# A mixer's masks and mean shift as matmuls, its state decay on ScalarE, and a last norm by pairs

## The chip, the cores and the metric

The kernel runs on one core of one Trainium2 chip. The metric is device time in microseconds (us) of one execution, the median over runs. Engines are named as the profile names them: PE (TensorE matmul), PEld (its weight load), DVE (VectorE), ACT (ScalarE), POOL (GpSimd), SP (SyncE, which here only issues DMAs).

## The reference

One inference step of a decoder trunk with two layers, for a prompt of 256 tokens and 8 decode streams of one token: 264 columns, model width 1024.

```python
def layer(x, ...):                                   # post-norm, DN_ALPHA = sqrt(2)
    h = layer_norm(DN_ALPHA * x + 0.5 * swiglu(x, f1g, f1u, f1d), ln1_g, ln1_b)
    mix, s_new, c_new, p_new = mixer(h, s0, conv_buf, pool_buf, ...)
    h = layer_norm(DN_ALPHA * h + mix, ln2_g, ln2_b)
    return layer_norm(DN_ALPHA * h + 0.5 * swiglu(h, f2g, f2u, f2d), ln3_g, ln3_b)
def mixer(h, ...):
    qkv, z, b_raw, a_raw, p = split(h @ w_in)        # q,k,v: 4 heads of 128 each; p: 4 groups of 128
    q, k, v = causal_conv(qkv, conv_buf, conv_w)     # 4 taps, then silu
    o, s_new = gated_delta(q, k, v, beta, g, s0)     # decay exp(g); dec = exp(gc_i - gc_j) for i >= j
    o_dn = rms_norm(o) * onorm_g * silu(z)
    y = (window_means(p, 2/4/8/16) - p) @ pool_w * pool_scale
    return concat([o_dn, y]) @ w_out, s_new, ...
```

The decode streams carry a 128x128 state for each head and stream: s_new = decay * s0 + (outer product).

## The kernel before

All activations lie transposed, channels on partitions and the 264 tokens along the free axis, in tiles of 128 channels. Weights come as fp32 and are used in two parts: for each 128x1024 piece ACT writes a rounded copy (`whi`, L178) and DVE the rest (`wlo`, L183); `mm3` (L219 to L221) multiplies in three matmuls per 128x128 block. Three slots each hold `whi` and `wlo`, so a piece is split when PE has left the piece three before it. PE runs in the order of the code; for the other engines a scheduler sets the order when the program is built, and each engine then works strictly in that order, waiting where a semaphore is not there yet.

A layer is: FFN (L428 on), norm, mixer (L495 on), norm, FFN, norm. The mixer, in PE's order:

- the k projections, the projections q0 and p3 with the small one for beta and decay, then q1, p2, q2, p1, `map3`, q3, the three `pdiff` products, p0, `map2`, v0, `map1`, v1, the transposes of k (`psq`), v2, `map0`, the mean shift `psh`, v3 with the scores (`psc`).
- `p_tile(g)` (L590) copies a pool projection into `ext`, and POOL builds the window sums `wsum` by g+1 additions of shifted copies (L604). `wsum` and `ext` have two buffers each: an addition must wait until the sum two before it is read.
- `p_map(g)` (L609) makes the row `dm` (mean less token) in four DVE steps, L615, L617, L619 and L620; its `finish`, called map3 to map0 here, multiplies it with the pool weights (`py`, L624). For g=3 alone `dm` is made without high priority.
- the decays: DVE makes four masked tiles `gm` (L702), PE sums them over tokens in `pdiff` (L706), ACT takes exp into `DT` (L708), and POOL multiplies `DT` by the causal mask or a factor (L710, L711).
- `conv` (L520): one ACT and three DVE steps per q, k or v tile (L525); `k_raw` keeps the k projections until then.
- then seven levels that invert a triangular matrix (`pP`, `pUt`, `pR` on PE, `QW`, `V`, `T` on DVE and ACT, `N` on POOL at L1008). Between the steps of a level PE does the z projections (`pz`), reads of the decode state (`psk`) and the first half of the output projection (`pop`). `decode_conv` (L776) prepares the decode keys, `less_shift` (L324) subtracts the mean shift from the residual X on POOL, `stack` (L902) splits the decode keys into the tile `parts` (L905 on ACT, L906 on POOL) and transposes it on PE (`pst`, L908), and POOL decays the state `S` (L885).

The lines of the pool means and of the decay masks that the rest of the text names:

```python
                    nx = mp.tile([P, EXT], F32, name="wsum", tag="wsum", bufs=2)
                    nc.gpsimd.tensor_add(nx[:, lo + d:], cur[:, lo + d:], cur[:, lo:EXT - d])
...
                with tc.high_priority() if g < 3 else nullcontext():
                    nc.vector.scalar_tensor_tensor(dm[:, 16:SEQ], cur[:, 31:15 + SEQ], 1.0 / wd, ext[:, 31:15 + SEQ],
                                                   ALU.mult, ALU.subtract)
                    nc.vector.scalar_tensor_tensor(dm[:, SEQ:], csm[:, :, 15], 1.0 / wd, smp[:, :, 15],
                                                   ALU.mult, ALU.subtract)
                    nc.vector.tensor_mul(dm[:, 0:16], cur[:, 15:31], cst[:, C_INV + 16 * g:C_INV + 16 * g + 16])
                    nc.vector.tensor_sub(dm[:, 0:16], dm[:, 0:16], ext[:, 15:31])
...
                        nc.vector.tensor_mul(gm, lemask, gp[:, i, t, :].unsqueeze(2).to_broadcast([P, H, P]))
```

The third step is the last that reads `wsum` (`cur`); the fourth reads `ext` alone.

After the last layer `output` (L379) subtracts the mean (`dmu`), multiplies by rstd and the gain, adds the bias, and stores y.

Of the kernel before, what the change touches and what calls it, by code (L numbers as in the profile page):

```python
# [25 lines left out]
H = 4  # L26
# [7 lines left out]
XB = 5  # L34
SB = 3
IDLE = 18

# [52 lines left out]
def trunk(ctx: ExitStack, tc: tile.TileContext, a: dict):  # L90
# [16 lines left out]
    onr = cpool.tile([P, P], F32R, name="onr")  # L107
    gto = cpool.tile([P, 2, P], F32R, name="gto")

    kq = cpool.tile([P, H * P], F32R, name="kq")  # L110
# [128 lines left out]
    class Norm:  # L239
# [78 lines left out]
        def centre(self):  # L318
            p = psa.tile([P, T], F32, name="psh", tag="ax")
            for k in range(2):  # L320
                nc.tensor.matmul(p, onr, HH[:, k, :], start=k == 0, stop=k == 1)
            self.set_shift(p, 4.0)

        def less_shift(self, after):  # L324
            for m in range(KD):
                with behind(after):
                    nc.gpsimd.tensor_sub(X[:, m, :], X[:, m, :], self.shift)  # L327

# [50 lines left out]
        def output(self, out):  # L379
            for m in (0, 1, 2, 3, 6, 7, 4, 5):  # L380
                y = X[:, m, :]
                (nc.gpsimd if m > 3 else nc.vector).tensor_sub(y, y, self.dmu)
            prev = None
            for m in (0, 1, 2, 3, 6, 4, 5, 7):
                y = X[:, m, :]
                if m > 5:
                    nc.gpsimd.tensor_mul(y, y, self.rstd)
                    with behind(prev):
                        nc.scalar.activation(y, y, AF.Identity, scale=self.g(m), bias=self.b(m))
                else:  # L390
                    nc.vector.scalar_tensor_tensor(y, y, self.g(m), self.rstd, ALU.mult, ALU.mult)
                    if m > 3:
                        nc.vector.tensor_scalar(y, y, self.b(m), None, ALU.add)
                    else:
                        prev = nc.scalar.activation(y, y, AF.Identity, bias=self.b(m))
                n = {4: 0, 6: 0, 5: 2, 7: 2}.get(m, 1)
                if n:
                    nc.sync.dma_start(out=out[(m - n + 1) * P:(m + 1) * P, :].rearrange("(m p) t -> p m t", p=P),
                                      in_=X[:, m - n + 1:m + 1, :])

# [94 lines left out]
    def mixer(l, src, norm, xstack):  # L495
        with tc.tile_pool(name="mp", bufs=1, reuse_waits="tile") as mp:
# [39 lines left out]
            def k_raw(ps):  # L536
                y, bias = src.settle(ps)
                raw = mp.tile([P, T], F32, name="raw", tag="tmp", bufs=4)
                nc.scalar.activation(raw, y, AF.Identity, bias=bias)
                return raw  # L540
# [25 lines left out]
            def q_tile(j, ps=None):  # L566
                W.ahead(2)
                conv(ps or product(W.get(), "q"), 4 + j)
                cq[j] = ct[4 + j]
# [39 lines left out]
            def p_map(g):  # L609
                ext, smp, cur = pend[g]  # L610
                wd = 2 << g
                dm = mp.tile([P, T], F32, name="dm", tag="tmp", bufs=4)
                csm = cur[:, 15 + SEQ:].rearrange("p (b i) -> p b i", i=16)
                with tc.high_priority() if g < 3 else nullcontext():
                    nc.vector.scalar_tensor_tensor(dm[:, 16:SEQ], cur[:, 31:15 + SEQ], 1.0 / wd, ext[:, 31:15 + SEQ],  # L615
# [6 lines that stand above are left out]
                def finish():  # L622
                    py = psa.tile([P, T], F32, name="py", tag="ax")
                    nc.tensor.matmul(py, pw[:, g, :], dm, start=True, stop=True)  # L624
                    yp = mp.tile([P, T], F32, name="yp", tag="tmp", bufs=4)
# [11 lines left out]
            p_tile(3, pp)  # L637
            for j in range(4):
                conv(kr[j], j)
            ck = ct[0:4]  # L640

# [3 lines left out]
            with tc.high_priority():  # L645
# [70 lines left out]
            v_tile(0, e_last)  # L716
            p_map(1)()

# [20 lines left out]
            for t in range(2):  # L739
                sumsq(ck, ssk, ke, t)  # L740
            v_tile(2, e_last)
# [4 lines left out]
            p_map(0)()  # L746
            norm.centre()
# [16 lines left out]
            v_tile(3, e_last, [nothing] * 2 + [lambda h=h: score(h) for h in range(H)])  # L764

            state = {}

# [8 lines left out]
            def decode_conv():  # L776
# [8 lines left out]
                nc.gpsimd.tensor_sub(lo, kq_in, hi.bitcast(F32))  # L785
                state["dsq"] = nc.gpsimd.tensor_mul(dsq[:, 8:12], dec[:, 0:4], dec[:, 4:8])
                nc.scalar.dma_start(out=a["o_ctail"][l], in_=stg)
# [56 lines left out]
            sk = dtile("sk", 2 * HB)  # L844
            skt = mp.tile([P, T], F32, name="skt", tag="tmp", bufs=4)[:, 0:P]

# [7 lines left out]
            def s_read(x):  # L854
# [18 lines left out]
                def last():  # L873
# [27 lines left out]

            def stack(i, src_, dst):  # L902
# [3 lines left out]
                nc.gpsimd.tensor_sub(pt[:, :, 2 - i, :], hb(src_), pt[:, :, 0, :])  # L906
                p = psa.tile([P, P], F32, name="pst", tag="ax")
                nc.tensor.transpose(p, parts[i], ident())  # L908
# [46 lines left out]
            def w_pool(m):  # L955
# [6 lines left out]
                def step(k):  # L962
                    mm3(ps, w, 4 * (m % 2) + k, mh[4 + k], ml[4 + k], k == 0, k == 3)

# [105 lines left out]
            for x in range(2):  # L1070
                pack(2, x)
            norm.less_shift(state["dsq"])
            for x in range(2):
# [14 lines left out]
            def stack_u():  # L1088
                stack(1, us, ust)
                s_prep(0)  # L1090
                s_prep(1)

            def w_level():
# [3 lines left out]
            fillers = [lambda: z_level(1, decode_sums, s_read(0), nothing),  # L1097
                       lambda: z_level(2, lambda: stack(0, dk, kst), s_read(1), nothing),
                       lambda: z_level(3, nothing, (s_turn, nothing), norms), q_level, w_level]
# [178 lines left out]
    def constants_in():  # L1278
        nc.sync.dma_start(out=sm, in_=a["small"])
        nc.sync.dma_start(out=cst, in_=a["cst"])  # L1280
        nc.scalar.activation(onr, cst[:, C_M1024:C_M1024 + P], AF.Copy)
        nc.scalar.activation(gto, cst[:, C_ONE:C_ONE + 2 * P].rearrange("p (i n) -> p i n", i=2), AF.Copy)
        for t in (*parts, kq.bitcast(F32)):
# [106 lines left out]
```

## Time and profile before

| | |
|---|---|
| three runs | 1083.95, 1085.35, 1085.57 us; median 1085.35 |
| profiled execution | 1089.43 us; its span 1087.6 us |
| PE busy in the span | 1046.0 us (96%) |
| DVE, ACT, POOL busy | 765.6, 581.8, 205.9 us |
| mean granted PE clock | 0.989 of full speed |

The span runs from the first to the last instruction; the profiled execution's own time holds 1.8 us more. An idle engine costs time only where the engine that ends the stretch waits for it, so the table alone says only that PE seldom waits.

### The profile page before, as it was taken

The page shows a single profiled execution, that of the slowest core. Times are in us where ns is not written, and L with a number is a line of the kernel's source. Part 1 is how long each engine was busy: PE and PEld are TensorE (multiplying, and loading weights), DVE is VectorE, ACT ScalarE, POOL GpSimd, SP SyncE. Part 2 cuts the span into 40 slices and gives each one's busy share as a digit, 9 for nine tenths or more (in the row PEclk, how much of TensorE's full clock was granted, in tenths as well). Part 3 has the DMA queues.
Part 4 walks back from the last instruction along what each step waited for, and adds up shares of the span by engine and source line. Part 5 has one row for each costly group of instructions (what it writes and reads, how often), then busy time and mean ns, then how long its engine had stood idle before and what let it go on. Part 6 is the DMA issues. An engine that isn't in the chain of part 4 may idle for free.

```text
span 1087.6 us, 20766 instructions
## 1 busy us (share of the span) xinstructions
PE 1046.0 (96%) x8410; PEld 1030.9 (95%) x8410; DVE 765.6 (70%) x1226; ACT 581.8 (53%) x1016; POOL 205.9 (19%) x248
## 2 busy tenths in 40 slices
PE   8999999998899999999999999999899999999995
PEld 8999999988798999999999999999788999999994
DVE  5555567899789955557785555778996898555554
ACT  6444445666447744444574444466664476444432
POOL 0000012244940000003200000322467300000132
PEclk9999999999999999999999999999999999999997
DMA  8554444732234355544725545565331345455441
GB/s 306 187 192 172 179 172 184 290 130 83 97 133 169 127 190 189 194 169 180 265 86 194 179 172 192 180 236 195 130 119 41 154 165 188 166 190 194 155 156 40
DMA packets 35872, 183.24 MB, mean 168 GB/s; under 512 B 6848, under 2 KB 12608, under 8 KB 15552
## 3 DMA queue, kind: packets, MB, share of 16 engines
q1 hardware_dynamic: 28704, 175.19, 44.6%
q10 hardware_dynamic: 7072, 6.72, 1.8%
q8 instruction: 66, 1.08, 0.4%
q14 instruction: 30, 0.25, 0.1%
HBM read 175.18 MB, written 6.72 MB: 167 GB/s over the span
## 4 chain that ended last, share of the span: by engine, by line
PE 82%; DVE 10%; ACT 3%; POOL 2%; issue 1%; DMA 1%; ACTq 0%; DVEq 0%
PE pd L219 8%; PE pd L221 8%; PE pd L220 8%; PE pu L220 8%; PE pu L219 8%; PE pu L221 8%; PE pg L220 7%; PE pg L219 7%; PE pg L221 7%; DVE wlo L183 2%; POOL X L327 1%; DVE c L525 1%; ACT X L367 1%; DMA wraw<-in_f_gu 1%; PE pout L220 1%
## 5 line engine op out<-in xcount | busy, mean ns | idle before, releaser
L183 DVE TENSOR_TENSOR wlo<-wraw,whi 128x1024 fp32r<-128x1024 f32 (+1 forms) x301 | 369.9, 1231 | 203.8 <-ACT whi L178 203.0
L178 ACT ACTIVATE whi<-wraw 128x1024 fp32r<-128x1024 f32 (+1 forms) x301 | 312.5, 1041 | 318.7 <-issue 116.9
L219 PE MATMUL pd<-gh,whi 128*128 128x264 f32 x704 | 200.6, 285 | 0.0
L221 PE MATMUL pd<-gh,wlo 128*128 128x264 f32 x704 | 200.2, 284 | 0.0
L220 PE MATMUL pd<-gl,whi 128*128 128x264 f32 x704 | 199.1, 283 | 0.0
L219 PE MATMUL pg<-HH,whi 128*128 128x264 f32 x632 | 179.8, 284 | 1.2 <-ACT whi L178 1.2
L221 PE MATMUL pg<-HH,wlo 128*128 128x264 f32 x632 | 179.6, 284 | 0.3 <-DVE wlo L183 0.3
L219 PE MATMUL pu<-HH,whi 128*128 128x264 f32 x632 | 179.5, 284 | 0.0
L220 PE MATMUL pg<-HL,whi 128*128 128x264 f32 x632 | 179.4, 284 | 0.0
L220 PE MATMUL pu<-HL,whi 128*128 128x264 f32 x632 | 179.2, 284 | 0.0
L221 PE MATMUL pu<-HH,wlo 128*128 128x264 f32 x632 | 179.2, 284 | 0.0
L220 PEld LDWEIGHTS pd<-gl,whi 128*128 128x128 f32 x704 | 132.6, 188 | 0.0
L221 PEld LDWEIGHTS pd<-gh,wlo 128*128 128x128 f32 x704 | 132.6, 188 | 0.0
L219 PEld LDWEIGHTS pd<-gh,whi 128*128 128x128 f32 x704 | 132.5, 188 | 0.0
L301 POOL TENSOR_TENSOR s<-X 128x264 fp32r<-128x264 f32 x4 | 3.0, 759 | 632.7 <-DVE X L298 632.7
L219 PEld LDWEIGHTS pg<-HH,whi 128*128 128x128 f32 x632 | 119.1, 188 | 1.5 <-ACT whi L178 1.4
L221 PEld LDWEIGHTS pg<-HH,wlo 128*128 128x128 f32 x632 | 118.6, 188 | 0.9 <-DVE wlo L183 0.7
L220 PEld LDWEIGHTS pg<-HL,whi 128*128 128x128 f32 x632 | 119.2, 189 | 0.1
L220 PEld LDWEIGHTS pu<-HL,whi 128*128 128x128 f32 x632 | 119.2, 189 | 0.0
L219 PEld LDWEIGHTS pu<-HH,whi 128*128 128x128 f32 x632 | 119.1, 189 | 0.0
L221 PEld LDWEIGHTS pu<-HH,wlo 128*128 128x128 f32 x632 | 118.5, 188 | 0.0
L439 DVE TENSOR_TENSOR gt<-sg,pu 128x264 f32<-128x264 f32 x79 | 33.9, 429 | 50.5 <-PE pu L221 50.5
(374 smaller groups left out, 2051.0 us busy)
## 6 DMA issues: line engine op xcount, KB each, us to landing
wraw<-in_f_gu SPq DMA_DIRECT2D x86, 1024.0 KB, 4.8
wraw<-in_f_d SPq DMA_DIRECT2D x44, 1024.0 KB, 4.8
wraw<-in_w_in SPq DMA_DIRECT2D x20, 1024.0 KB, 5.0
wraw<-in_w_out SPq DMA_DIRECT2D x8, 1024.0 KB, 4.8
S<-in_sdelta SPq DMA_DIRECT2D x8, 512.0 KB, 6.2
out_o_ds<-S ACTq DMA_DIRECT2D x8, 512.0 KB, 2.6
X<-in_xT ACTq DMA_DIRECT2D x4, 264.0 KB, 5.4
wraw<-in_f_gu SPq DMA_DIRECT2D x4, 256.0 KB, 7.1
```

Of the source, the lines that this page charges most:

```text
L178: self.last_hi = nc.scalar.activation(h, r, AF.Copy)
L183: nc.vector.tensor_sub(l, r, h.bitcast(F32))
L219: nc.tensor.matmul(ps, hi[:, k, :], xh, start=first, stop=False)
L220: nc.tensor.matmul(ps, hi[:, k, :], xl, start=False, stop=False)
L221: nc.tensor.matmul(ps, lo[:, k, :], xh, start=False, stop=last)
L301: nc.gpsimd.tensor_add(self.s2, X[:, 0, :], X[:, 1, :])
L327: nc.gpsimd.tensor_sub(X[:, m, :], X[:, m, :], self.shift)
L367: nc.scalar.activation(X[:, m, :], X[:, m, :], AF.Identity, scale=self.g(m), bias=self.b(m))
L439: nc.vector.tensor_mul(gt, sg, u)
L525: nc.vector.scalar_tensor_tensor(c[:, d:SEQ], y[:, 0:SEQ - d], cw(j, 3 - d), c[:, d:SEQ], ALU.mult, ALU.add)
```

## The change

- **Masks.** The two masked `DT` tiles get a third matmul that adds -16384 where the mask is zero, so exp gives 0; the third tile's factor becomes two more matmuls. The three POOL multiplications go: `pdiff` has 10 matmuls, before 6.
- **Shift.** The mean shift is kept as one row (`less`), and each of the eight `pop` products starts with a matmul of one row of ones by it. POOL's eight subtractions from X go.
- **State decay.** POOL's eight multiplications of 128x512 per layer become 32 of 128x128 on ACT.
- **Decode keys.** Their split into `parts` moves from `stack` to `decode_conv`.
- **Key convolutions.** The four k convolutions stand between q1, p2, q2 and q3's places instead of all behind p3; a q tile asks for weights four pieces ahead, before two.
- **Pool means.** `dm` gets two buffers of its own; `yp`, `raw` and `skt` move to the pool that holds the norms' squares. `map1` is called behind `psq` and `map0` behind v3.
- **Output.** The last norm works on pairs of tiles: the mean is read from PSUM by DVE for six tiles, POOL subtracts for two, ACT does gain and bias for six, DVE for two, and four stores of a pair each take the place of six.

```diff
-            self.set_shift(p, 4.0)
-        def less_shift(self, after):
-            for m in range(KD):
-                with behind(after):
-                    nc.gpsimd.tensor_sub(X[:, m, :], X[:, m, :], self.shift)
+            self.less = lpool.tile([P, T], F32R, name="less", tag="shift")[0:1]
+            nc.scalar.activation(self.less, p[0:1], AF.Copy, scale=-4.0 * ALPHA)
+        def less_shift(self, ps):
+            nc.tensor.matmul(ps, gto[0:1, 0], self.less, start=True, stop=False)
...
         def output(self, out):
+            by2 = lambda v: v.unsqueeze(1).to_broadcast([P, 2, T])
+            pairs = [X[:, m:m + 2, :] for m in range(0, KD, 2)]
+            for n, y in enumerate(pairs):
+                if n < 3:
+                    nc.vector.tensor_sub(y, y, by2(self.mean))
+                else:
+                    for m in (6, 7):
+                        nc.gpsimd.tensor_sub(X[:, m, :], X[:, m, :], self.dmu)
+            for n, y in enumerate(pairs):
+                nc.vector.tensor_mul(y, y, by2(self.rstd))
+                for m in (2 * n, 2 * n + 1):
+                    if n < 3:
+                        nc.scalar.activation(X[:, m, :], X[:, m, :], AF.Identity, scale=self.g(m), bias=self.b(m))
+                    else:
+                        nc.vector.tensor_scalar(X[:, m, :], X[:, m, :], self.g(m), self.b(m), ALU.mult, ALU.add)
+                nc.sync.dma_start(out=out[2 * n * P:2 * (n + 1) * P, :].rearrange("(m p) t -> p m t", p=P), in_=y)
...
             def q_tile(j, ps=None):
-                W.ahead(2)
+                W.ahead(4)
...
-                dm = mp.tile([P, T], F32, name="dm", tag="tmp", bufs=4)
+                dm = mp.tile([P, T], F32, name="dm", tag="dm", bufs=2)
...
             q_tile(0, pq)
             p_tile(3, pp)
-            for j in range(4):
-                conv(kr[j], j)
-            ck = ct[0:4]
...
+            conv(kr[0], 0)
             q_tile(1)
+            conv(kr[1], 1)
             p_tile(2)
+            conv(kr[2], 2)
             q_tile(2)
+            conv(kr[3], 3)
+            ck = ct[0:4]
...
+            upper = gto[:, 1].unsqueeze(1).to_broadcast([P, H, P])
             for j, (t, msk) in enumerate(((0, gto[:, 1]), (1, gto[:, 0]), (1, gto[:, 1]))):
                 pd = psa.tile([P, H, P], F32, name="pdiff", tag="ax")
-                for i in range(2):
-                    nc.tensor.matmul(pd, msk, gms[t, i], start=i == 0, stop=i == 1)
-                dt = DT[:, :, j * P:(j + 1) * P]
-                e_last = nc.scalar.activation(dt, pd, AF.Exp)
-                if j != 1:
-                    nc.gpsimd.tensor_mul(dt, dt, lemask)
-            nc.gpsimd.tensor_mul(DT[:, :, P:2 * P], DT[:, :, P:2 * P], DT[:, :, P - 1:P].to_broadcast([P, H, P]))
+                steps = [(msk, gms[t, i]) for i in range(2)]
+                if j == 1:
+                    steps += [(gto[:, 1], gms[0, i][:, :, P - 1:P].to_broadcast([P, H, P])) for i in range(2)]
+                else:
+                    steps.append((far, upper))
+                for i, (st, mv) in enumerate(steps):
+                    nc.tensor.matmul(pd, st, mv, start=i == 0, stop=i == len(steps) - 1)
+                e_last = nc.scalar.activation(DT[:, :, j * P:(j + 1) * P], pd, AF.Exp)
...
             v_tile(0, e_last)
-            p_map(1)()
+            map1 = p_map(1)
...
+                in_parts(0, dk)
+                nc.gpsimd.tensor_mul(dsq[:, 8:12], dec[:, 0:4], dec[:, 4:8])
...
                     for h in range(H):
-                        s = Ss[h][:, 4 * x:4 * x + 4, :]
-                        nc.gpsimd.tensor_mul(s, s, ab[:, h * NB + 4 * x:h * NB + 4 * x + 4].unsqueeze(2)
-                                             .to_broadcast([P, 4, P]))
+                        for b in range(4 * x, 4 * x + 4):
+                            s = Ss[h][:, b, :]
+                            nc.scalar.activation(s, s, AF.Copy, scale=ab[:, h * NB + b:h * NB + b + 1])
```

What the scheduler made of it shows best on DVE, around the `gm` tiles of the first mixer. Before, the row `dm` of group 3 (here dm_2869) stands complete ahead of `gm`; "waits" names the engines and queues whose semaphores a row needs:

```order
L615 SCALAR_TENSOR_TENSOR dm_2869<-wsum_2689,ext_2677 128x240 [waits Pool_49]
L667 SCALAR_TENSOR_TENSOR p__2728<-p__2728,s__2726 128x12 [waits DVE_49]
L617 SCALAR_TENSOR_TENSOR dm_2869<-wsum_2689,ext_2677 128x8 [waits DMAHW3_49]
L619 TENSOR_TENSOR dm_2869<-wsum_2689,cst_72 128x16
L669 SCALAR_TENSOR_TENSOR xa_2724<-p__2728,xa_2724 128x12 [waits DVE_49]
L183 TENSOR_TENSOR wlo_2877<-wraw_2874,whi_2876 128x1024 [waits DMAHW6_49,PE_49,Activation_49]
L671 TENSOR_TENSOR gg_2748<-xa_2724,nega_2721 128x12 [waits DVE_49]
L620 TENSOR_TENSOR dm_2869<-dm_2869,ext_2677 128x16
L183 TENSOR_TENSOR wlo_2879<-wraw_2874,whi_2878 128x1024 [waits PE_49,Activation_49]
L702 TENSOR_TENSOR gm_2962<-cst_72,gp_2752 128x512 [waits Activation_49]
L702 TENSOR_TENSOR gm_2966<-cst_72,gp_2752 128x512
```

In the changed program, at the same place, the group-3 row is dm_2881 (its first and largest step stands ahead of `gg`, in rows not shown), the group-2 row is dm_2968, and c6 is a key convolution:

```order
L524 SCALAR_TENSOR_TENSOR c6_2869<-pq_2844,sm_73,c6_2869 128x254 [waits DVE_49]
L703 TENSOR_TENSOR gm_2976<-cst_72,gp_2740 128x512 [waits DVE_49]
L703 TENSOR_TENSOR gm_2980<-cst_72,gp_2740 128x512
L524 SCALAR_TENSOR_TENSOR c6_2869<-pq_2844,sm_73,c6_2869 128x253 [waits DVE_49]
L616 SCALAR_TENSOR_TENSOR dm_2881<-wsum_2701,ext_2689 128x8 [waits DMAHW3_49]
L618 TENSOR_TENSOR dm_2881<-wsum_2701,cst_72 128x16
L185 TENSOR_TENSOR wlo_2930<-wraw_2927,whi_2929 128x1024 [waits DMAHW7_49,PE_49,Activation_49]
L614 SCALAR_TENSOR_TENSOR dm_2968<-wsum_2826,ext_2791 128x240 [waits Pool_49]
L616 SCALAR_TENSOR_TENSOR dm_2968<-wsum_2826,ext_2791 128x8 [waits DMAHW5_49]
L618 TENSOR_TENSOR dm_2968<-wsum_2826,cst_72 128x16
L619 TENSOR_TENSOR dm_2881<-dm_2881,ext_2689 128x16 [waits DVE_49]
```

So three of the four steps of the group-3 row now stand behind all four `gm`, and the last of them also behind a weight piece and three steps of the group-2 row, which wait for POOL. On PE, meanwhile, the product with the group-3 row stands where it stood, behind p1 and ahead of q3 and `pdiff`. The changed program there:

```order
L223 MATMUL pp_2889<-HH_75,wlo_2678 128x264
L623 MATMUL py_2921<-dm_2881,pw_2395 128x264 [waits DMAHW2_49,DVE_49,PE_49]
L221 MATMUL pq_2937<-HH_75,whi_2836 128x264 [waits PE_49,Activation_49]
L222 MATMUL pq_2937<-HL_76,whi_2836 128x264
L223 MATMUL pq_2937<-HH_75,wlo_2837 128x264
L221 MATMUL pq_2937<-HH_75,whi_2836 128x264
```

The first product that PE cannot start without DVE is thus `py` of group 3; `pdiff`, 24 matmuls further on, waited for DVE before and now has no wait of its own left. On POOL, before, behind the decode convolution (`dec`):

```order
L778 TENSOR_TENSOR dec<-ptmp,pre 128x96
L781 TENSOR_TENSOR dsq<-dec 128x64
L786 TENSOR_TENSOR dsq<-dec 128x32
L327 TENSOR_TENSOR X<-X,shift 128x264
L785 TENSOR_TENSOR kq<-dec,kq 128x4x16
L327 TENSOR_TENSOR X<-X,shift 128x264 x7
L1008 TENSOR_TENSOR N<-MT,cst 128x128 x4
L906 TENSOR_TENSOR parts_82<-dec,parts_82 128x4x8
```

and in the changed program:

```order
L783 TENSOR_TENSOR dec<-ptmp,pre 128x96
L786 TENSOR_TENSOR dsq<-dec 128x64
L792 TENSOR_TENSOR dsq<-dec 128x32
L790 TENSOR_TENSOR kq<-dec,kq 128x4x16
L912 TENSOR_TENSOR parts_83<-dec,parts_83 128x4x8
L1018 TENSOR_TENSOR N<-MT,cst 128x128 x16
```

Eight subtractions and four `N` no longer stand ahead of `parts`, and no decay of `S` stands among the `N`.

On ACT all 32 decays of a layer's `S` now stand within two of the seven levels, among the steps `V` and `QW` and the copies `RH` of the state, which `psk` on PE reads. The changed program there, from the end of one level into the next:

```order
L892 ACTIVATE S<-S,ab 128x128 x4
L1052 ACTIVATE V_3294<-T_3292 128x256 [waits DVE_49]
L892 ACTIVATE S<-S,ab 128x128 x4
L1052 ACTIVATE V_3295<-T_3293 128x256 [waits DVE_49,Activation_49]
L892 ACTIVATE S<-S,ab 128x128 x3
L817 ACTIVATE zs<-pz 128x264 [waits PE_49]
L917 ACTIVATE kst<-pst 128x128 [waits PE_49]
L856 ACTIVATE RH<-S 128x2x256 [waits PE_49,Activation_49]
L1059 ACTIVATE QW_3296<-pUt 128x256 [waits PE_49]
L856 ACTIVATE RH<-S 128x2x256 [waits Activation_49]
L892 ACTIVATE S_3282<-S_3282,ab 128x128 x4
L892 ACTIVATE S<-S,ab 128x128 x4
```

Eleven decays stand ahead of the first of these two `RH`, and five more ahead of those, from the first `V` of the level before on, where twelve other steps stand as well: four `V`, four `RH`, two `QW`, `zs` and `kst`. On PE, `psk` with the first of these `RH` comes behind `pP`, `pUt` and one block of `pz` of the new level; a whole level has eight such blocks of three matmuls, eight `psk` of 512 columns, two `pP`, two `pR` and two `pUt`.

## Rows read from the trace of the kernel before

**Rows 1.** The page: busy time by engine.

```profile
PE 1046.0 (96%) x8410; PEld 1030.9 (95%) x8410; DVE 765.6 (70%) x1226; ACT 581.8 (53%) x1016; POOL 205.9 (19%) x248
```

**Rows 2.** Windows: stretch, PE, PEld, DVE, ACT, POOL busy, PEclk, DMA, GB/s.

```profile
14.00:200.00 186.00, 185.91 (x1536) 185.91 (x1537) 114.34 (x136) 92.63 (x134) 16.46 (x16) 1.00 0.54 199
...
250.00:260.00 10.00, 7.25 (x46) 7.22 (x47) 8.59 (x21) 7.16 (x18) 1.60 (x2) 0.83 0.31 113
...
285.00:290.00 5.00, 5.00 (x28) 4.82 (x28) 1.56 (x4) 1.47 (x4) 5.00 (x7) 0.70 0.00 0
```

**Rows 3.** Waits of PE: us in total, times, longest.

```profile
PE py L624 <- DVE dm L620: 6.2, 2, 3.2
PE pst L908 <- POOL parts L906: 5.6, 2, 2.8
...
PE pdiff L706 <- DVE gm L702: 2.1, 2, 1.2
...
PE pp L221 <- DVE wlo L183: 1.2, 2, 0.6
...
PE psk L861 <- DVE RL L851: 1.0, 3, 0.4
```

**Rows 4.** Timeline of PE, first layer: map3, `pdiff`, a level, `pst` (start, length).

```profile
236.40 0.68 PE L624 MATMUL py<-dm,pw 128*128 128x264 f32 x2 [0.26 <-PE pp L221]
...
241.47 1.74 PE L706 MATMUL pdiff<-gm,gto 128*128 128x512 f32 x5 [1.25 <-DVE gm L702]
...
280.35 0.61 PE L1025 MATMUL pP<-T,N 128*128 128x128 f32 x4
280.79 0.38 PE L1047 MATMUL pUt<-cst,V 128*128 128x128 f32 x2
280.93 0.37 PE L219 MATMUL pz<-HH,whi 128*128 128x264 f32 x1
...
284.79 0.47 PE L908 MATMUL pst<-cst,parts 128*128 128x128 f32 x1 [2.81 <-POOL parts L906]
```

**Rows 5.** Timeline of DVE around `gm`, first layer.

```profile
236.22 1.21 DVE L183 TENSOR_TENSOR wlo<-wraw,whi 128x1024 fp32r<-128x1024 f32 x1
237.35 2.58 DVE L702 TENSOR_TENSOR gm<-cst,gp 128x512 fp32r<-128x512 f32 x2
...
240.74 0.67 DVE L702 TENSOR_TENSOR gm<-cst,gp 128x512 fp32r<-128x512 f32 x1
```

**Rows 6.** Timeline of POOL: window sums beside those rows, and ahead of `parts`.

```profile
234.40 3.73 POOL L604 TENSOR_TENSOR wsum<-wsum 128x396 f32<-128x396 f32 x2 [2.89 <-DVE xa L669]
...
273.91 7.44 POOL L327 TENSOR_TENSOR X<-X,shift 128x264 f32<-128x264 f32 x7
```

**Rows 7.** Tile `wsum`: ns of one, least, median, most.

```profile
L604 POOL TENSOR_TENSOR wsum<-wsum x12: 840/1108/1868, 224.2 to 774.6; 128x396 f32<-128x396 f32 x6, 128x392 f32<-128x392 f32 x4, 128x384 f32<-128x384 f32 x2
```

**Rows 8.** Timeline of ACT: copies among the levels, and 128x128 steps elsewhere.

```profile
288.81 0.63 ACT L850 ACTIVATE RH<-S 128x512 fp32r<-128x512 f32 x1 [3.24 <-PE psk L861]
289.35 0.40 ACT L1042 ACTIVATE V<-T 128x256 f32<-128x256 f32 x1
289.65 0.62 ACT L850 ACTIVATE RH<-S 128x512 fp32r<-128x512 f32 x1
...
328.97 1.12 ACT L1173 ACTIVATE on<-po,fr 128x128 f32<-128x128 f32 x4
```

**Rows 9.** Line 362, a pair of tiles less the mean from PSUM: ns of one.

```profile
L362 DVE TENSOR_TENSOR X<-X,ps x20: 693/700/705, 206.6 to 891.1; 128x528 f32<-128x528 f32 x20
```

**Rows 10.** Timeline of DVE, then ACT, in the tail.

```profile
1074.67 2.73 DVE L382 TENSOR_TENSOR X<-X,dmu 128x264 f32<-128x264 f32 x3
...
1079.01 0.43 DVE L130 SCALAR_TENSOR_TENSOR rstd<-lnv,rstd 128x264 f32<-128x264 f32 x1
1079.48 3.48 DVE L391 SCALAR_TENSOR_TENSOR X<-X,sm,rstd 128x264 f32<-128x264 f32 x6
...
1082.62 1.09 ACT L389 ACTIVATE X<-X,sm 128x264 f32<-128x264 f32 x2
```

More of the change, by code (lines that the diff above doesn't have):

```diff
@@ L35 @@
 SB = 3
+FAR = 16384.0
 IDLE = 18
@@ L108, in trunk @@
     gto = cpool.tile([P, 2, P], F32R, name="gto")
+    far = cpool.tile([P, P], F32R, name="far")
     kq = cpool.tile([P, H * P], F32R, name="kq")
@@ L379, in output @@
         def output(self, out):
[L380 to L389, printed above, removed]
-                else:
-                    nc.vector.scalar_tensor_tensor(y, y, self.g(m), self.rstd, ALU.mult, ALU.mult)
-                    if m > 3:
-                        nc.vector.tensor_scalar(y, y, self.b(m), None, ALU.add)
-                    else:
[L395 to L399, printed above, removed]
+            by2 = lambda v: v.unsqueeze(1).to_broadcast([P, 2, T])
[3 more added lines that the diff above has]
+                    nc.vector.tensor_sub(y, y, by2(self.mean))
+                else:
+                    for m in (6, 7):
[5 more added lines that the diff above has]
+                        nc.scalar.activation(X[:, m, :], X[:, m, :], AF.Identity, scale=self.g(m), bias=self.b(m))
+                    else:
+                        nc.vector.tensor_scalar(X[:, m, :], X[:, m, :], self.g(m), self.b(m), ALU.mult, ALU.add)
+                nc.sync.dma_start(out=out[2 * n * P:2 * (n + 1) * P, :].rearrange("(m p) t -> p m t", p=P), in_=y)
         def raw_products(self, nms, steps):
@@ L537, in k_raw @@
                 y, bias = src.settle(ps)
-                raw = mp.tile([P, T], F32, name="raw", tag="tmp", bufs=4)
+                raw = lpool.tile([P, T], F32, name="raw", tag="sq", bufs=4)
                 nc.scalar.activation(raw, y, AF.Identity, bias=bias)
@@ L624, in finish @@
                     nc.tensor.matmul(py, pw[:, g, :], dm, start=True, stop=True)
-                    yp = mp.tile([P, T], F32, name="yp", tag="tmp", bufs=4)
+                    yp = lpool.tile([P, T], F32, name="yp", tag="sq", bufs=4)
                     nc.scalar.activation(yp, py, AF.Copy, scale=sm[:, l, S_PS + g:S_PS + g + 1])
@@ L740, in mixer @@
                 sumsq(ck, ssk, ke, t)
+            map1()
             v_tile(2, e_last)
@@ L745, in mixer @@
                 nc.vector.tensor_mul(wsc, wsc, beta[:, 0:2, :])
-            p_map(0)()
+            map0 = p_map(0)
             norm.centre()
@@ L764, in mixer @@
             v_tile(3, e_last, [nothing] * 2 + [lambda h=h: score(h) for h in range(H)])
+            map0()
             state = {}
@@ L785, in decode_conv @@
                 nc.gpsimd.tensor_sub(lo, kq_in, hi.bitcast(F32))
-                state["dsq"] = nc.gpsimd.tensor_mul(dsq[:, 8:12], dec[:, 0:4], dec[:, 4:8])
+                in_parts(0, dk)
+                nc.gpsimd.tensor_mul(dsq[:, 8:12], dec[:, 0:4], dec[:, 4:8])
                 nc.scalar.dma_start(out=a["o_ctail"][l], in_=stg)
@@ L844, in mixer @@
             sk = dtile("sk", 2 * HB)
-            skt = mp.tile([P, T], F32, name="skt", tag="tmp", bufs=4)[:, 0:P]
+            skt = lpool.tile([P, T], F32, name="skt", tag="sq", bufs=4)[:, 0:P]
             def s_split(h, x):
@@ L900, in mixer, with in_parts @@
             ust = mp.tile([P, P], F32R, name="ust")
-            def stack(i, src_, dst):
+            def in_parts(i, src_):
                 pt = parts[i].rearrange("p (h r b) -> p h r b", h=H, b=NB)
@@ L906, in stack @@
                 nc.gpsimd.tensor_sub(pt[:, :, 2 - i, :], hb(src_), pt[:, :, 0, :])
+            def stack(i, dst):
                 p = psa.tile([P, P], F32, name="pst", tag="ax")
@@ L962, in step @@
                 def step(k):
-                    mm3(ps, w, 4 * (m % 2) + k, mh[4 + k], ml[4 + k], k == 0, k == 3)
+                    if k == 0:
+                        norm.less_shift(ps)
+                    mm3(ps, w, 4 * (m % 2) + k, mh[4 + k], ml[4 + k], False, k == 3)
                 def add(after=None):
@@ L1071, in mixer @@
                 pack(2, x)
-            norm.less_shift(state["dsq"])
             for x in range(2):
@@ L1088, in stack_u @@
             def stack_u():
-                stack(1, us, ust)
+                in_parts(1, us)
+                stack(1, ust)
                 s_prep(0)
@@ L1097, in mixer @@
             fillers = [lambda: z_level(1, decode_sums, s_read(0), nothing),
-                       lambda: z_level(2, lambda: stack(0, dk, kst), s_read(1), nothing),
+                       lambda: z_level(2, lambda: stack(0, kst), s_read(1), nothing),
                        lambda: z_level(3, nothing, (s_turn, nothing), norms), q_level, w_level]
@@ L1281, in constants_in @@
         nc.scalar.activation(onr, cst[:, C_M1024:C_M1024 + P], AF.Copy)
+        nc.scalar.activation(far, cst[:, C_ID:C_ID + P], AF.Copy, scale=-FAR)
         nc.scalar.activation(gto, cst[:, C_ONE:C_ONE + 2 * P].rearrange("p (i n) -> p i n", i=2), AF.Copy)
```

## The prediction

> **What bounds the kernel now.** The page first: PE is busy 96% of the span, DVE 70%, ACT 53%, POOL 19% [rows 1]. In the windows an FFN stretch holds 1536 matmuls in 186 us without a gap, 0.121 us per 264 columns; that sets the price of added PE work (512 columns: 0.235). So time is won or lost where PE waits. The list of PE's waits names few places, nearly all in the two mixers: `py` on `dm`, `pst` on POOL's `parts`, `pdiff` on `gm`, `pp` on a weight piece, `psk` on DVE [rows 3]. Each of the two long waits costs more than itself: the windows behind them show a granted clock of 0.83 over 10 us and 0.70 over 5 us, that is 1.7 and 1.5 us lost to 1.2 GHz after PE had stood idle [rows 2]. The rest is the tail, where PE is done and DVE, ACT and POOL finish the last norm [rows 10].
>
> I work with the first layer's clock times; the second repeats them. The profiled execution took 1089.4 us, 4.1 above the median, so I sum differences and put them on the median, 1085.35.
>
> **The wait for `pst` goes.** PE waits 2.81 us for `parts`, twice [rows 3, 4], because POOL does seven subtractions from X (7.44 us [rows 6]) and four `N` first. In the changed order `parts` stands right behind the decode convolution, and on POOL only `N` is left behind it. The wait and the slow clock go: −2.8 − 1.5 = **−4.3** per layer. What could be late next is `N`, which stands earlier now too.
>
> **A wait for `py` of map3 comes.** The order shows three of the four steps of its `dm` behind four `gm`, the last also behind a weight piece and behind three steps of the group-2 row, which wait for POOL's second and third sum. These in turn need the buffer that the group-3 row's third step frees. So one chain runs DVE, POOL, DVE, with PE at its end.
> - PE reaches `py` at 236.40 − 0.61 (the `pp` wait, whose weight piece now comes ahead of this stretch) = 235.8 [rows 3, 4].
> - DVE starts `gm` at 236.1 to 237.3; before it was 237.35, with one more weight piece ahead [rows 5]. Four `gm` at 0.60 (0.67 less the overlap with the next; POOL is idle then), two convolution steps of half as many columns at 0.4, and short steps for 0.3 as an estimate: the third step is done at 239.6 to 240.8.
> - Two sums take 1.7 (the least, 0.84 each [rows 7]) to 3.7 (before, beside DVE's two-input steps [rows 6]). One weight piece of 1.2 lies beside them, so I take 2.7: 242.3 to 243.5.
> - Four steps of the two rows, 0.6: `py` at 242.9 to 244.1. I take 243.3, an idle of 7.5; the ends with the sums' bounds are 241.9 and 245.1, 6.1 to 9.3.
> Then the slow clock, 1.7 as after the 3.2 us wait. Against it go the waits that stood here: `pp` 0.6, `pdiff` 1.2 (second layer 0.9), `py` of map1 3.2 (3.0) with its slow clock 1.7 [rows 2, 3], since `map1` is called behind `psq` and DVE has the idle of PE to catch up. `pdiff` itself has ten matmuls at 0.235, 2.3, where before six went at 0.32 (five in 1.74 with the overlap [rows 4]), 1.9, as `gm` came one by one: +0.4. Net 7.5 + 1.7 + 0.4 − 6.7 = +2.9, and +3.4 in the second layer, **+6.3** for both layers; bounds +3.5 and +9.9. If `py` of map1 still waits, 3 more.
>
> **The shift by matmul.** Eight products of one row by 264 columns at 0.121: **+1.0** per layer. PE is on the path there, so nothing hides it.
>
> **The decays on ACT.** 32 of 0.25 each (four 128x128 steps in 1.12 with the overlap to the next [rows 8]) are 8 us per layer. From the first `V` of a level to the first `RH` of the next ACT now does four `V` at 0.30, five `RH` at 0.54 to 0.63, two `QW` as `V`, `zs` and `kst` at 0.25: 5.1, which before fitted. With 16 decays it is 9.1. PE needs that `RH` after one level of work, counted from its own `V`: eight `pz` blocks at 0.36, eight `psk` at 0.235, four `pP` or `pR` at 0.44 and two `pUt` at 0.14 [rows 4] are 6.9, and half a microsecond more, 7.4. So `psk` is late by some 1.6; if ACT starts that `V` early, by nothing. The `psk` waits of before (1.0 in both layers) go, as POOL no longer runs beside `RL`. I take **+1.0** net per layer; bounds −0.5 and +2.
>
> **The other edits.** Weights four pieces ahead and convolutions in other places are hidden under the projections, where PE had no wait but 0.6; uncovered they would add at most a convolution step or two, 0.8. The `ext` loads of groups 1 and 0 stand behind two more weight loads on SP; their `map1` and `map0` are called later too, by 24 matmuls (2.9 us) and more.
>
> **The tail.** Before, `rstd` ended at 1079.4 and the last gain step at 1083.7, 4.3 later [rows 10]. Now DVE starts its three paired subtractions at 1074.7: three at 0.70 [rows 9] and three steps of the chain at 0.43 end at 1078.1. A paired multiplication (0.70, same size) and six ACT steps of 0.54 follow: 1082.0; DVE's share, four pairs and two short steps, ends at 1081.5. **−1.7**. The bound: before, three subtractions beside POOL took 2.73, 0.91 each against 0.42 alone; if POOL's two (1.7 us) slow the pairs likewise, 1.0 of it is lost, −0.7.
>
> The Trainium skill ("SBUF — State Buffer", section "Who interferes with whom") states that a DVE instruction with two SBUF inputs and a GpSimd instruction that reads SBUF exclude each other for the whole instruction, and that one with at most one SBUF input does not contend. The slow subtractions of before, with both inputs in SBUF, agree. The paired ones take the mean from PSUM, so by the page the tail gains the full 1.7; by the rows of before alone it is anything from 0.7.
>
> **Sum.** −8.6 + 6.3 + 2.0 + 2.0 − 1.7 = 0.0 us: the level of before. The decays' bounds for both layers, −1 to +4, have their middle at 1.5, below the 2.0 taken, as ACT may begin that `V` early: with 1.5 the sum is −0.5, and I say **1084.8**.
>
> **The rivals.**
> *DVE comes through early, faster.* Without POOL's `DT` products beside it DVE's two-input steps run at their undisturbed times throughout; `py` of map3 starts at 241.9, the sums take 1.7, ACT's decays sit in idle ACT time. Map3 nets +3.5, decays −1.0: −8.6 + 3.5 + 2.0 − 1.0 − 1.7 = −5.8, 1079.5. For it: ACT was busy about half of the span [rows 1]. Against it: the decays stand in clumps of four to eleven.
> *The decays land on the inversion, slower.* V and QW wait behind clumps of up to 11 decays (2.75 us), and PE stands in several places, so that half of the 8 us shows: +4 per layer for 1, so 1091. From 2.1 us per layer on it ends slower than before by more than 0.2%. Against it: the steps between leave PE other work.
> *The map3 chain is longer, slower.* Sums at 3.7 and `gm` at 1.29 as in the rows beside POOL, and `py` of map1 waits again: +9.9 + 3 instead of 6.3, so 1092. It decides from an idle of 8.6 us on, in both layers. Against it: POOL has nothing else to do there.
> *The `pst` wait doesn't go.* `parts` needs the decode convolution, which waits for the last v tile; PE may then wait at `pds` in place of `pst`. Half of the 8.6 stays: 1089.7. Against it: the subtractions that go, which stand between `dsq` and `parts`, are alone 7.4 us [rows 6].
>
> **How the numbers follow.** About 0.2% (2.2 us) is what a measurement of this kernel can tell from no change: 1083.2 to 1087.5. The forecast case (1081.5 to 1088) gets 0.45; early DVE (1077 to 1082) 0.27; decays on the inversion 0.11; a longer map3 chain 0.11; `pst` not freed 0.06. A quarter of the forecast case lies below 1083.2 and a twentieth above 1087.5: faster 0.27 + 0.12 = 0.39, level 0.32, slower 0.28 + 0.01 = 0.29. The range 1078.0 to 1090.0 leaves out some 0.07 below, in the early case, and 0.13 above, in the two slower ones.
>
> **What would show it.** Right: no wait of `pst` over 0.5 us; a wait of `py` on `dm` of 6 to 9 us at map3 in both layers, and none at `pdiff` or map1; `psk` waits behind `RH` of 1 to 2 us; paired subtractions at 0.70 and the last DMA 1.7 us nearer to PE's end. Wrong: a `py` wait under 5 us or over 10; waits of `pUt` or `pR` on ACT; a wait at `pds`.

## The result, and the profile after

The changed kernel takes 1093.56 us (median of 4 runs, 1093.05 to 1094.32) against 1084.65 of the kernel before (4 runs): ratio 1.0085, 95% interval 1.0068 to 1.0103. It is slower, by 0.7% to 1.0%; 1084.8 was predicted, with a range of 1078 to 1090.

The size needs one more sentence. The runs of the kernel before spread from 1081.65 to 1093.3 us, with granted clocks from 0.995 down to 0.987. On a chip that had 22 of them beside 6 more of the changed kernel the medians are 1088.96 and 1093.59, ratio 1.0044 (1.0027 to 1.0061). So the first four runs of before lay low in a wide spread, and about 5 us is the better measure of the loss. The two profiled executions differ by that too: spans 1087.6 and 1092.5.

The changed kernel's page, busy time and the chain that ended last:

```profile
PE 1052.6 (96%) x8434; PEld 1035.2 (95%) x8434; DVE 749.3 (69%) x1223; ACT 597.9 (55%) x1081; POOL 156.7 (14%) x206
...
PE 88%; ACT 4%; DVE 4%; issue 2%; DMA 1%; ACTq 0%; DVEq 0%
```

POOL lost 49 us, DVE 16, ACT gained 16, and PE 6.6 busy us beside [rows 1]. PE's waits, of the whole span:

```profile
PE py L623 <- issue: 18.4, 2, 9.2
...
PE psk L867 <- DVE RL L857: 0.7, 2, 0.4
```

`pst`, `pdiff` and `pp` are gone from this list [rows 3], `psk` is 0.7 where it was 1.0, and one long wait has come: `py`, 9.2 us in each layer. ("issue" stands there as the semaphore's release isn't seen; the DVE rows below show it.) The windows answer [rows 2]:

```profile
14.00:200.00 186.00, 185.95 (x1537) 185.95 (x1538) 114.41 (x135) 93.18 (x135) 16.46 (x16) 1.00 0.54 200
240.00:250.00 10.00, 5.82 (x25) 5.64 (x26) 5.07 (x19) 1.36 (x4) 4.58 (x6) 0.51 0.15 47
250.00:260.00 10.00, 10.00 (x74) 9.53 (x74) 3.60 (x10) 9.67 (x23) 0.85 (x1) 1.00 0.32 113
285.00:290.00 5.00, 5.00 (x40) 4.72 (x39) 2.95 (x8) 5.00 (x18) 1.56 (x3) 1.00 0.00 0
```

The FFN is as it was, and both stretches that had run slowly are at full clock, but from 240 to 250 all of PE's work goes at 0.51: 25 matmuls in ten microseconds. How map3 came there, on DVE, then POOL and PE:

```profile
238.79 1.27 DVE L703 TENSOR_TENSOR gm<-cst,gp 128x512 fp32r<-128x512 f32 x2
...
240.47 0.15 DVE L618 TENSOR_TENSOR dm<-wsum,cst 128x16 f32<-128x16 f32 x1
240.55 1.21 DVE L185 TENSOR_TENSOR wlo<-wraw,whi 128x1024 fp32r<-128x1024 f32 x1
243.42 0.41 DVE L614 SCALAR_TENSOR_TENSOR dm<-wsum,ext 128x240 f32<-128x240 f32 x1 [1.66 <-POOL wsum L603]
...
243.91 0.17 DVE L619 TENSOR_TENSOR dm<-dm,ext 128x16 f32<-128x16 f32 x1
...
240.76 2.62 POOL L603 TENSOR_TENSOR wsum<-wsum 128x396 f32<-128x396 f32 x2 [9.28 <-DVE dm L618]
...
244.18 1.22 PE L623 MATMUL py<-dm,pw 128*128 128x264 f32 x2 [9.20 <-issue]
```

That is the chain of the prediction, step for step: third step, two sums on POOL, three steps of the other row, fourth step, `py`.

Where the time went in the first layer is read from three places of PE's timeline: the first `psq`, the second scores `psc`, and the first product of the next FFN, `pg`. Before:

```profile
257.73 1.03 PE L729 MATMUL psq<-cst,c 128*128 128x128 f32 x8
...
299.45 0.60 PE L751 MATMUL psc<-c,c 128*128 128x256 f32 x2
299.88 0.39 PE L752 MATMUL psc<-c,c 128*128 128x128 f32 x2
300.02 0.37 PE L219 MATMUL pop<-RH,whi 128*128 128x264 f32 x1
300.23 0.28 PE L220 MATMUL pop<-RL,whi 128*128 128x264 f32 x1
...
345.27 0.28 PE L219 MATMUL pg<-RH,xhi 128*128 128x266 f32 x1
```

and after:

```profile
261.65 1.03 PE L732 MATMUL psq<-cst,c 128*128 128x128 f32 x8
...
299.54 0.70 PE L755 MATMUL psc<-c,c 128*128 128x256 f32 x2 [0.18 <-ACT QW L1059]
300.07 0.38 PE L756 MATMUL psc<-c,c 128*128 128x128 f32 x2
300.39 0.38 PE L329 MATMUL pop<-less,gto 1*128 1x264 f32 x1
300.70 0.39 PE L221 MATMUL pop<-RH,whi 128*128 128x264 f32 x1
300.93 0.28 PE L222 MATMUL pop<-RL,whi 128*128 128x264 f32 x1
...
348.28 0.29 PE L221 MATMUL pg<-RH,xhi 128*128 128x266 f32 x1
```

The first stretch loses 3.9 us, the second gains it back (41.72 us before, 37.89 after), and the third, where nobody waits, loses 2.9 (45.82 and 48.74). In the second layer the three are 4.4, 3.5 and 2.9. The tail, from DVE's `var` to the end of the span, gives 2.1 (13.3 us before, 11.2 after). The third stretch is the surprise, and the rows show where: from the second `psc` matmul to the second matmul of the weight block are 0.35 us before and 0.86 after. The one-row matmul (1*128) starts 0.32 behind its forerunner, where 0.14 was usual, and the next starts 0.31 behind it. A 264-column matmul should have added 0.12; this adds 0.5, eight times a layer.

### The profile page after: what moved, and what is told of

Same layout as the page of the kernel before. It is cut to its first block, busy times and chain, and to the rows that moved or that the text cites. A ratio compares the mean times of both kernels' runs of the same rounds, so it can differ in the third digit from the quotient of the medians.

```text
span 1092.5 us, 20801 instructions
## 1 busy us (share of the span) xinstructions
PE 1052.6 (96%) x8434; PEld 1035.2 (95%) x8434; DVE 749.3 (69%) x1223; ACT 597.9 (55%) x1081; POOL 156.7 (14%) x206
## 4 chain that ended last, share of the span: by engine, by line
PE 88%; ACT 4%; DVE 4%; issue 2%; DMA 1%; ACTq 0%; DVEq 0%
PE pd L221 8%; PE pd L223 8%; PE pd L222 8%; PE pu L222 8%; PE pu L221 8%; PE pu L223 8%; PE pg L222 7%; PE pg L221 7%; PE pg L223 7%; ACT S L892 2%; PE pop L221 1%; ACT X L369 1%; PE pout L222 1%; PE psc L755 1%; DMA wraw<-in_f_gu 1%
```

## The experiments

The changed kernel stands for 1093.6 below. It was measured again beside the middle four experiments only; the first four and the last four ran on two other chips, where the medians of the kernel before were 1088.4 and 1088.0 (1089.0 in the middle group). So a few tenths between groups mean nothing, and the stretches of the traces are given where they decide.

**Full rows.** Same order on every engine; only the operand's shape differs.

```diff
-            self.less = lpool.tile([P, T], F32R, name="less", tag="shift")[0:1]
-            nc.scalar.activation(self.less, p[0:1], AF.Copy, scale=-4.0 * ALPHA)
+            self.less = lpool.tile([P, T], F32R, name="less", tag="shift")
+            nc.scalar.activation(self.less, p, AF.Copy, scale=-4.0 * ALPHA / P)
-            nc.tensor.matmul(ps, gto[0:1, 0], self.less, start=True, stop=False)
+            nc.tensor.matmul(ps, gto[:, 0], self.less, start=True, stop=False)
```

> The changed kernel, with the shift row kept on all 128 partitions (divided by 128, which is exact) and multiplied by the full matrix of ones; instructions and order stay the same on every engine. Theory A, the one-row form is dear: in the trace of the changed kernel each of the 16 products spends 0.49 us more ahead of its first weight block than before, against 0.12 for a full matmul of 264 columns; full rows give back 16 x 0.37 = 5.9 us: about 1087.7. Theory B, any matmul more at the head of a product costs that, whatever its rows: no change, 1093.6.

1089.53 (12 runs, 1088.68 to 1090.3): 4.1 less. The timeline of PE at the same place:

```profile
299.77 0.70 PE L755 MATMUL psc<-c,c 128*128 128x256 f32 x2 [0.18 <-ACT QW L1059]
300.30 0.38 PE L756 MATMUL psc<-c,c 128*128 128x128 f32 x2
300.44 0.37 PE L329 MATMUL pop<-less,gto 128*128 128x264 f32 x1
300.65 0.28 PE L221 MATMUL pop<-RH,whi 128*128 128x264 f32 x1
300.77 0.29 PE L222 MATMUL pop<-RL,whi 128*128 128x264 f32 x1
...
346.56 0.29 PE L221 MATMUL pg<-RH,xhi 128*128 128x266 f32 x1
```

The head takes 0.47 in place of 0.86, 16 x 0.39 = 6.2 us. Theory A holds, B falls. The third stretch is 46.79 us, 1.95 less than in the changed kernel and 0.97 more than before: with full rows the term costs the +1.0 per layer that the prediction gave it. Of the 6.2 some 2 come back as waits that the slow heads had covered (`pku` on `vt` 0.27, a gap of 0.35 ahead of the second `pout` in the first layer).

PE's weight loads show the difference too. Here the load for the first block behind the head starts at 300.53, 0.12 ahead of its matmul. In the changed kernel the load of the one-row matmul and the one behind it start only with their matmuls, at 300.39 and 300.70.

**Two one-row matmuls of half the shift.**

```diff
+            for i in range(2):
+                nc.tensor.matmul(ps, gto[0:1, 0], self.less, start=i == 0, stop=False)
```

> The changed kernel with two one-row matmuls of half the shift in place of each one. Theory A1, the change between one row and 128 rows is what costs: the second stands beside the first and adds 0.12 us each, 16 x 0.12 = 1.9 us: 1095.5. Theory A2, each one-row matmul costs by itself, 0.31 to 0.49 us: 5 to 8 us more, 1098.6 to 1101.6.

1094.1 (12 runs): 0.5 more, far from A2 and less than the 1.9 of A1; the third stretch grew by 0.5 in the first layer. The rows:

```profile
298.83 0.38 PE L757 MATMUL psc<-c,c 128*128 128x128 f32 x2
299.14 0.50 PE L330 MATMUL pop<-less,gto 1*128 1x264 f32 x2
299.57 0.39 PE L221 MATMUL pop<-RH,whi 128*128 128x264 f32 x1
299.80 0.28 PE L222 MATMUL pop<-RL,whi 128*128 128x264 f32 x1
```

Two take 0.43 to the next matmul where one took 0.31: the second costs the usual 0.12, its weight load (two are in the trace) included. So what is dear is the change of shape, into one row and out of it, and not the matmul.

**All four rows of means at high priority.**

```diff
-                with tc.high_priority() if g < 3 else nullcontext():
+                with tc.high_priority():
```

> The changed kernel with all four rows of pool means at high priority, so that the group-3 row stands ahead of the gm tiles on DVE. Theory: the wait of 9.2 us at map3 and the slow clock behind it (about 2.5 us) go in both layers, and at most 3 us per layer come back at pdiff or another py: 14 to 23 us less, 1071 to 1080. Rival: DVE is short of time in this stretch whatever its order, so that 5 us of waits per layer come back as they stood in the kernel before, with slow clock: 1080 to 1086.

1088.07 (12 runs): 5.5 less, outside both ranges: waits came back, as the rival had it, but more than either said. The wait at map3 is gone and another has come, in the list of PE's waits:

```profile
PE pdiff L713 <- DVE gm L703: 11.1, 4, 3.2
```

The row of DVE's timeline that makes the longer of the first layer's two:

```profile
243.65 0.41 DVE L614 SCALAR_TENSOR_TENSOR dm<-wsum,ext 128x240 f32<-128x240 f32 x1 [1.67 <-POOL wsum L603]
```

The group-1 row, urgent as it was in the changed kernel, now stands between the second and the third `gm` and waits for POOL.

**Both edits.**

> Full rows and the group-3 row at high priority together. The two stand in different stretches of the mixer, so the gains should add: e1 plus e3, that is 5.9 us less than e3 by theory A. If they do not add, one of them hides waits that the other brings out.

1084.26 (12 runs): 9.3 less than the changed kernel, 4.1 + 5.5 = 9.6 expected from the two single runs (by theory A's 5.9 it was 1082.2). They add.

**The changed kernel again.**

> The changed kernel once more, beside the others of this call on the same chip: 1093.0 to 1094.3 as before; it is what the next three are compared with.

1093.59 (6 runs), as told above.

**Weights two pieces ahead, as before.**

```diff
             def q_tile(j, ps=None):
-                W.ahead(4)
+                W.ahead(2)
```

> The changed kernel with a q tile asking for weights two pieces ahead, as before the change. In the order the second and third step of the group-3 row then stand ahead of gm, and POOL's sums come free earlier; the fourth step stays behind the four gm. Theory, the place of these steps in DVE's order makes the map3 wait, and asking for weights further ahead moved them: the wait shrinks from 9.2 to some 6.5 us in each layer, 5 to 6 us less in all: 1088. Rival, asking further ahead is worth something by itself (a weight piece comes earlier): no gain, or slower than 1093.6.

1088.14 (11 runs), as the theory has it, and the wait is the predicted one:

```profile
PE py L623 <- issue: 13.7, 2, 6.9
```

So the load edit, which moves no arithmetic, had moved two steps of the row behind `gm`, and that cost 5.4 us.

**The group-3 row alone at high priority, with full rows.**

```diff
-                with tc.high_priority() if g < 3 else nullcontext():
+                with tc.high_priority() if g == 3 else nullcontext():
```

> Full rows of the shift, and the priority turned round: the group-3 row alone at high priority, the other three without. In the order the group-3 row stands early, the four gm follow with no wait for POOL ahead of them, and the group-2 row comes behind two weight pieces. Theory, the wait of map3 and the gm wait of the run with all rows at high priority both come from a wait for POOL ahead of gm in DVE's order: both go, what stays is at most 1.5 us per layer at pdiff, without slow clock; 2 x 4 to 2 x 6 us less than with all rows at high priority: 1072 to 1077. Rival, DVE has too much work ahead of gm in any order: 1081 to 1084.

1076.19 (4 runs, 1075.79 to 1077.63), ratio to before 0.9889 (0.9862 to 0.9916). In the first layer DVE's last wait for POOL ends at 228.5, ten us ahead of `gm`. What is left in PE's list is 2.4 per layer, where at most 1.5 was expected:

```profile
PE pdiff L713 <- DVE gm L703: 4.7, 4, 1.7
```

and the windows, at full clock:

```profile
230.00:245.00 15.00, 12.21 (x86) 11.05 (x85) 15.00 (x33) 7.78 (x20) 4.00 (x4) 1.00 0.47 155
245.00:260.00 15.00, 14.56 (x116) 14.19 (x116) 14.03 (x35) 14.06 (x33) 1.81 (x3) 1.00 0.43 151
```

The version with all rows urgent and full rows, with the same steps on DVE, took 1084.26. It is the place in DVE's queue, not the amount of DVE's work.

**The shift on POOL again.** The eight subtractions and `behind(after)` of the kernel before, no one-row matmul; all else as changed.

> The changed kernel with the mean shift subtracted on POOL again (eight subtractions per layer, behind the decode products) and no one-row matmul; the decode keys' split stays where the change put it, ahead of four of the subtractions. Theory, the early split alone frees pst and the one-row matmuls only cost: 16 x 0.49 = 7.8 us less, 1086. Rival, POOL must be rid of the subtractions too, else N is late and PE waits at pP in place of pst: 2.8 us and slow clock come back in each layer, and the result is 1093 to 1095.

1089.48 (11 runs): between the two. No wait of `pst` or `pP` is in PE's list, so the rival's mechanism falls, and the early split alone had freed `pst`. But only half of the 7.8 us shows: PE's list has a wait of `pout` on DVE again (0.6 in each layer, as in the kernel before), and from `psq` to `psc` PE takes 0.8 us longer. As full rows give 1089.53, these runs show no gain of the matmul over POOL's subtraction (from `psq` to `pg` PE takes 84.7 us with full rows and 84.8 here, in the first layer).

**The kernel before again, with a profile.**

> The kernel before, once more with a profile. Its runs lie between 1081.7 and 1093.3 us with granted clocks of 0.995 to 0.987, where the changed kernel's lie within 2.3 us. Theory, its waits of 2.8 to 3.2 us at pst and map1 end now ahead of and now behind the fall of the clock: in a profile with a time near 1082 the windows behind those waits show full clock, in one near 1089 they show 0.70 to 0.89 as in the rows of before. Rival, the waits themselves differ from run to run: their lengths differ by a microsecond or more.

1088.86 (10 runs, 1082.37 to 1091.02). The profiled execution took 1089.1, so no early one was caught; but its second layer tells the theories apart. Its `pst` in the timeline:

```profile
818.88 0.33 PE L908 MATMUL pst<-cst,parts 128*128 128x128 f32 x1 [2.81 <-POOL parts L906]
```

Its window around that wait:

```profile
817.50:821.50 4.00, 2.62 (x20) 2.54 (x21) 1.84 (x4) 0.31 (x2) 4.00 (x5) 1.00 0.00 0
```

The same window of the first profile of before, where this place lies 1.5 us earlier:

```profile
817.50:821.50 4.00, 4.00 (x20) 3.91 (x21) 1.04 (x3) 0.41 (x2) 4.00 (x6) 0.63 0.00 0
```

The wait is 2.81 us in both, followed by full clock in one and by 0.63 in the other. In the first layer of this same execution it is 2.81 us again, with the matmuls behind it 0.22 apart where 0.121 is full speed. The rival holds in part too: `py` of map1 waited 3.9 us at the longest here, 3.2 there [rows 3]. Which of the two makes most of the spread stays open, as no profile of an early execution was had.

**The old tail.**

> The changed kernel with the last norm as it was before. Theory, the pairs give 1.7 to 2.0 us, as the two profiles' tails differ by 1.9: 1095.3 to 1095.6. Rival, the tail's end is set by the stores and not by the arithmetic: 1093.6.

1095.76 (6 runs): 2.2 more, and 2.1 in the traces, from `var` to the end. The pairs are worth that.

**The decays on POOL again, in the changed kernel and in the best one.**

```diff
-                        for b in range(4 * x, 4 * x + 4):
-                            s = Ss[h][:, b, :]
-                            nc.scalar.activation(s, s, AF.Copy, scale=ab[:, h * NB + b:h * NB + b + 1])
+                        s = Ss[h][:, 4 * x:4 * x + 4, :]
+                        nc.gpsimd.tensor_mul(s, s, ab[:, h * NB + 4 * x:h * NB + 4 * x + 4].unsqueeze(2)
+                                             .to_broadcast([P, 4, P]))
```

> The changed kernel with the state's decay on POOL again, eight multiplications of 128x512 per layer. Theory, the decays fill ACT (14.9 us of the 15 from 285 to 300) but PE waits there for 0.7 us per layer only: at most 1.4 us less, 1092.2 to 1093.6. Rival as predicted: psk is late by 1 us and more per layer because of them: 1091.6 or less.

> The version with full rows and the group-3 row first (1076.2), with the state's decay on POOL again. If ACT's decays cost PE anything once the earlier waits are gone, this is faster than 1076; if POOL beside DVE's two-input steps costs more, slower. I expect 1075 to 1077.

1091.73 (11 runs), 1.9 less; and 1073.77 (6 runs, 1073.12 to 1075.31), 2.4 less than 1076.19 and below the 1075 expected at the least, ratio to before 0.9883 (0.9855 to 0.9912): the fastest version here. Both differences go across chips, but the traces bear them out: in the changed kernel from `psq` to `psc` 37.26 us in place of 37.89 and from `psc` to `pg` 48.38 in place of 48.74, 1.0 per layer.

So the size in the rival of the first expectation, which is the prediction's own term, is right. Its mechanism is not shown: PE's wait of `psk` is 0.8 us in both layers with the decays on POOL and 0.7 with them on ACT. What the changed kernel has more, from `psq` to `psc`, are two waits of PE's weight loads:

```profile
PEld psc L755 <- ACT QW L1059: 0.4, 1, 0.4
PEld psk L867 <- ACT RH L856: 0.3, 1, 0.3
```

The 0.4 behind `psc` stays unexplained. A window of the second stretch, of the changed kernel run again (PE's busy time stands third, ACT's sixth):

```profile
285.00:300.00 15.00, 14.34 (x107) 12.87 (x105) 9.37 (x21) 14.91 (x45) 4.95 (x9) 1.00 0.00 1
```

The same window with the decays on POOL, PE at 14.87 and ACT at 8.61:

```profile
285.00:300.00 15.00, 14.87 (x115) 13.83 (x114) 12.62 (x25) 8.61 (x20) 13.80 (x18) 1.00 0.18 64
```

## Why the prediction was wrong, point by point

- **The shift by matmul, +1.0 per layer: the step that failed.** It took a matmul of one row at the 0.121 us of 264 columns. The mechanism, PE work in a stretch where nobody waits, was right; the term measured 2.9 per layer between `psc` and `pg`, in heads that are 0.5 longer each (8 x 0.5 = 4.1), some 1.2 of it in place of waits that stood there. Both layers: 5.8 for 2.0. The form of the operand changes the price, and with full rows the term would have held (+0.97). The trace of before had a row that told it, a product of 8 rows:

```profile
272.89 0.61 PE L1035 MATMUL pR<-QW 128*128 128x128 f32 x4
273.43 0.43 PE L836 MATMUL pa<-ad,cst 8*128 8x64 f32 x2
273.79 0.46 PE L839 MATMUL pds<-dsq,cst 128*128 128x96 f32 x2
```

  From `pR` to `pa` are 0.54 where four `pR` take 0.36 to a `pz`, and the two `pa` of 64 columns take 0.36 where two `pUt` of 128 take 0.14 [rows 4]: about 0.4 for a change into few rows and out again. Eight of those are 3.2 us per layer, an estimate near what was measured.
- **The wait of map3, +2.9 and +3.4: right in kind, 1 us short each.** PE came to `py` at 235.0 (244.18 less 9.20; 235.8 predicted) and the row was done at 244.1 (243.3 taken, 245.1 the end of the bounds): 9.2 for 7.5, inside 6.1 to 9.3; 0.8 of the difference is PE's earlier coming, which costs nothing. The slow clock behind it cost more than behind a 3 us wait: 24 matmuls of q3 from 244.8 to 250.2 at 0.22 each are 2.4 us above 0.121, where 1.7 was taken. The waits that were to go all went. To `psq` it is 3.9 in the first layer and 4.4 in the second.
- **`pst`, −4.3, and the decays, +1.0: right in size.** Together −3.3 was predicted from `psq` to `psc`, −3.8 and −3.5 measured; the decays alone are 1.9 for both layers (2.0 predicted). But `psk` was to wait 1 to 2 us behind `RH` and its old waits were to go: it waits 0.35 per layer with the decays on ACT and 0.4 with them on POOL. So the decays' number is in part luck. And the subtractions did not have to leave POOL for `pst`: with them back, its wait stayed away.
- **"The other edits are hidden, at most 0.8": wrong for the loads.** Asking four pieces ahead cost 5.4 us, by way of DVE's order. The sum had the wait itself from the order, so no term was missed, but its cause was, and with it what would mend it.
- **The tail, −1.7: right**; 2.1 in the profiles, 2.2 by the old tail. The changed kernel's rows show three pairs in 1.31 + 0.69 and `rstd` at 1084.7, 3.1 behind the first subtraction, 3.4 predicted:

```profile
1081.66 1.31 DVE L387 TENSOR_TENSOR X<-X,ps 128x528 f32<-128x528 f32 x2
1082.89 0.43 DVE L130 TENSOR_TENSOR lnv<-var,rstd 128x264 f32<-128x264 f32 x1
1083.24 0.69 DVE L387 TENSOR_TENSOR X<-X,ps 128x528 f32<-128x528 f32 x1
...
1084.31 0.43 DVE L132 SCALAR_TENSOR_TENSOR rstd<-lnv,rstd 128x264 f32<-128x264 f32 x1
```

  POOL subtracted two tiles beside them, from 1081.6 to 1083.0, and did not slow the pairs (0.70 [rows 9]). The Trainium skill ("SBUF — State Buffer", "Who interferes with whom") states that a DVE instruction with at most one SBUF input, outside the 2-port perf modes, does not contend with GpSimd; these rows agree.
- **The base.** The sum, 0.0, was put on the median of three runs, 1085.35; the profile it was made from took 1089.4, and the wider samples say 1088 to 1089. With that base and the two terms above (+3.8 for the shift, +2 for map3) it comes to 1094. So some 3 us of the miss are the base and 3.8 the shift.
- **The rivals.** None had the shift dearer. The longer map3 chain was to decide from an idle of 8.6 us on, and the idle was 9.2; but its sums took 2.6 and not 3.7, its `gm` 0.64 and not 1.29, and map1 did not wait. That the time came near its 1092 is luck.

## What to carry to other kernels

A matmul with few rows is not a small matmul: spread the operand over all partitions, scaled so that the full sum is the same, before you mix it into a stream of full ones. A wait for another engine in a queue is paid by everything behind it, so look in the new order for each wait on a slow engine and ask what PE needs behind it; a priority, or a load that is asked for earlier, can put it there. A share of the chain is not a gain: the decays' line had 1.6% of the changed kernel's chain, 17 us, and taking them off ACT gave 1.9.

## What the hardware showed that was not expected

- A change between 128-row and one-row matmuls costs: starts 0.32 apart into the one-row form (0.14 usual), 0.31 on the way out and 0.23 to the next (0.21 and 0.12 behind a full one). The Trainium skill ("TensorEngine Tiling (Array Packing)", "Key Properties") states that changing the tiling mode drains TensorE. The runs with full rows and with two one-row matmuls would fit that; whether a one-row matmul counts as another tiling mode, no run here shows.
- The same wait of 2.81 us was followed by 2.4 GHz throughout in one execution (window at 1.00) and by a fall to 1.2 GHz in another (0.63). Whether such waits make the spread of the kernel before was not settled; the two versions with the group-3 row first, and the changed one, repeat within 2.3 us.
- A sum on POOL beside a weight piece on DVE took 1.70 us; the next, with DVE idle, took 0.84, the least [rows 7].
